# A transformer block on one core: a new opening of the first matrix product, and three due times moved

## The chip, the cores and the metric

The kernel runs on one core of one Trainium2 chip. The time is device microseconds of one launch, from start to end, the median of several runs. Engines are TensorE (PE; its weight loads are shown as PEld), VectorE (DVE), ScalarE (ACT), GpSimd (POOL) and SyncE (SP), which only issues transfers here.

## The reference

One layer on 256 tokens of width 2048: a gated feed-forward part, a mixer, and a second feed-forward part, each with a norm ahead and a norm behind, added to the stream.

```python
f = _swiglu(_rmsnorm(h, ln_ffn1_pre), ffn1_gate, ffn1_up, ffn1_down)
h = h + 0.5 * _rmsnorm(f, ln_ffn1_post)
mx = _hybrid_mixer(_rmsnorm(h, ln_mix_pre), ...)
h = h + _rmsnorm(mx, ln_mix_post)
f = _swiglu(_rmsnorm(h, ln_ffn2_pre), ffn2_gate, ffn2_up, ffn2_down)
h = h + 0.5 * _rmsnorm(f, ln_ffn2_post)
```

The mixer multiplies by `w_in` (columns for an RWKV-7 branch, a pooling branch and two gates). The RWKV branch is a recurrence over tokens with a 64x64 state for each of 16 heads. The pooling branch takes moving means over windows of 2, 4, 8 and 16 tokens, subtracts the input and multiplies each of four groups by a 256x256 matrix (the pool mix). Both branches go through a projection, are gated, added and multiplied by `w_out`. All is float32.

## The kernel before, in words

**Products.** A float32 product is made of three passes at the reduced type fp32r: each operand is split into a high part (ACT casts it: `wH`, `xH`) and the remainder (DVE subtracts: `wL`, `xL`), and TensorE adds H·H, L·H and H·L (lines 155 to 157, function `mm3`). One call of `mm3` for one slice k of 128 rows of the weight, 512 columns of output and one half h (128 tokens) is called a step here ("do" in the code). A product with 2048 rows has 16 slices and two halves, 32 steps. Weights come by SP in tiles of two slices (`get_w`, line 117), are split by `two` (lines 131 and 132), and the split tiles have five buffers; the loaded ones have four. Where the output is wanted transposed, 256-column matmuls are used (`ch_g`, line 311, tile name `mc`).

**Activations.** The right-hand sides must have the channel on the partition axis. `transpose_split` turns a 128x512 block of one half by four TensorE transposes against the identity (line 339, tile `tr`); ACT scales and casts each quarter (line 345) and DVE takes the remainder (line 347). Block c of half h serves slices 4c to 4c+3 of that half.

**The head** (`head`, called by the first `gemm_tok`) is the first product of the first feed-forward part. There the order on TensorE, ACT, DVE and SP is written out by hand: `load(h, c)` asks for a block of x, `load(None, None)` for the norm's gain row g1, which TensorE turns into a column; `get(k, n)` asks for weights, `split(k)` splits them, `turn(h, c)` is `transpose_split`, `do(k, h)` is a step. All asks are in SP's queue.

**Row ends.** `post` makes the last product of each part, then the norm behind it. In the last row of four (c = 3) its steps are queued half by half, with events put among them by their due times on a planned clock (`s.at`, `s.now`; `run` executes the queue). After half h ends, DVE multiplies the four quarters by the norm's factor and adds the stream (line 450, tile `fg`), and each quarter is then turned for the next part. `TURNS[h][q]` is the planned delay, in us after the half's end, of the transposes of quarter q. Steps of the next part's first product (`by_half`, half 0 first, ten slices) are queued behind and fill the time. `TURNS` is used after the first feed-forward part and after the mixer; after the last part there is nothing to turn.

**The mixer** orders TensorE by hand, the other engines' order is chosen by a scheduler. `rwkv` is a generator that yields numbers: how many us of other products (`fill`, from `rest`) are to be woven in at that place (`weave`); what one place draws more than it asked for is taken off the next. It runs for two halves of the heads. `fill` begins with what is left of `p_g`: the steps of a gate (`gb_g(1)`), of which 22 come ahead of the mix of the fourth pool group, `pool_mix(3)`, which needs `mxT` (split by ACT, line 751, and DVE, line 752) and its own weight. The recurrence has four chunks of 64 tokens: `pU`, copied by ACT; `pSa`, copied by DVE and ACT (lines 1044 and 1045); `pS`, from which DVE makes the next state (lines 1055 and 1056) that the next chunk's `pU` needs; and `pY`. Between pSa and pS stands `yield 1.7`. After the last chunk `pT` turns the result, which DVE and ACT split into yH and yL; the first 16 steps of the projection that follows use the other half's.

Of the kernel before, what the change touches and what calls it, by code (L numbers as in the profile page):

```python
# [18 lines left out]
P = 128  # L19
# [21 lines left out]
STAG = 10  # L41
TRAIL = 16
AHEAD = (5.0, 6.0)
TURNS = [[4.2, 5.3, 6.4, 7.5], [4.0, 5.0, 6.2, 7.4]]
TB = 4

ROWS = [("ln_mix_pre", 16), ("ln_ffn2_pre", 16), ("mu", 26), ("w0", 8), ("a0", 8),
# [4 lines left out]
class Block:  # L52
# [154 lines left out]
    def head(s, w, c0, KT, do, keep, xs):  # L207

        load, turn = xs
        w32 = {}  # L210

        def get(k, n):
            w32[k] = (n, s.get_w(w, k, n, c0, 512, own=True))

        def split(k):
            n, t = w32[k]
            keep(s.two(t, k, n, 512))
        E = mybir.EngineType
        with s.tc.manual_schedule(engines={E.PE, E.Activation, E.DVE, E.SP}):
            load(None, None)  # L220
            load(0, 0)
            get(0, 1)
            get(1, 1)
            load(1, 0)
            get(2, 1)
            get(3, 1)
            for c in range(1, 4):
                load(0, c)
                get(4 * c, 2)
                load(1, c)  # L230
                get(4 * c + 2, 2)
            split(0)
            turn(0, 0)
            split(1)
            do(0, 0)
            turn(1, 0)
            split(2)
            do(1, 0)
            split(3)
            do(0, 1)  # L240
            do(1, 1)
            do(2, 0)
            do(2, 1)
            for c in range(4):
                k = 4 * c
                if c < 3:
                    turn(0, c + 1)
                    split(k + 4)
                if c:
                    for i in range(3):  # L250
                        do(k + i, 0)
                        do(k + i, 1)
                        if c < 3 and i == 1:
                            turn(1, c + 1)
                            split(k + 6)
                elif c < 3:
                    turn(1, c + 1)
                    split(k + 6)
                do(k + 3, 0)
                do(k + 3, 1)  # L260
            s.stats()

    def stats(s):
# [90 lines left out]
    def turn(s, T1, h, src):  # L354

        s.nc.vector.transpose(out=T1[:, h * 512:h * 512 + 512], in_=src)  # L356
# [46 lines left out]
    def post(s, wd, at, KT, gpost, fac, resid, emit, reload):  # L403
# [11 lines left out]
        for c in range(4):  # L415
# [32 lines left out]
            def out(h, q, r, end):  # L448
                o = cc_(fg[h], q)
                nc.vector.scalar_tensor_tensor(out=o, in0=o, scalar=r, in1=resid(h, q),  # L450
                                               op0=ALU.mult, op1=ALU.add)
                emit(h, q, o, end + TURNS[h][q])
            s.gemm_tok(wd, c * 512, at, KT, ev, trail=(c == 3))
# [96 lines left out]
    def mixer(s, prm, uT, rs, resid, emit, gpost, reload):  # L550
        nc = s.nc
# [13 lines left out]
        for h in range(2):  # L565
            t = s.tmp("rb")
            nc.vector.tensor_copy(t[:, :P], rs[h].to_broadcast([P, P]))
            ps = s.psum("rb")
# [73 lines left out]
        def p_g():  # L642
            mix = None
            for g, win in enumerate(POOL_WINDOWS):
                mxT = s.unit((P, 2, 2, S), F32R, "mxT")
                yield from s.pool_window(g, win, at, w_in, mxT)
                if g:
                    yield from s.pool_mix(g - 1, mix, prm["pool_w"], pT)
                mix = mxT
            yield None  # L650
            gate = gb_g(1)
            for t in itertools.islice(gate, 22):
                yield t
            yield from s.pool_mix(3, mix, prm["pool_w"], pT)
            yield from gate
# [116 lines left out]
    def rwkv(s, hf, z, lz, prm, yH, yL):  # L772
        nc = s.nc
# [32 lines left out]
        k, v = z["k"], z["v"]  # L806
# [8 lines left out]
        for q in range(2):  # L815
            ps = s.psum("pw").rearrange("p (i t) -> p i t", i=2)
# [5 lines left out]
        for q in range(2):  # L822
            ps = s.psum("pa").rearrange("p (i t) -> p i t", i=2)
# [25 lines left out]
        ps = s.psum("pn")  # L849
# [16 lines left out]
        for pr in range(2):  # L866
            yield 3
            pss = []
            for src in (v, vs):
                ps = s.psum("pV").rearrange("p (i c) -> p i c", i=4)  # L870
# [3 lines left out]
            for b in range(2):  # L874
                c = 2 * pr + b
# [4 lines left out]
        for q in range(2):  # L880
            ps = s.psum("pk").rearrange("p (i t) -> p i t", i=2)
# [44 lines left out]
        for q in range(2):  # L926
            ar, bk = AR[q], BK[q]
            for i in range(2):
# [8 lines left out]
                for h, R, RK in ((0, E, O), (1, O, E)):  # L937
                    ps = pAs[h]
# [59 lines left out]
        ps = s.psum("pM").rearrange("p (g t) -> p g t", g=16)  # L998
# [8 lines left out]
        ps = s.psum("pX").rearrange("p (g t) -> p g t", g=16)  # L1007
# [18 lines left out]
        for c in range(NCH):  # L1026
            yield 1.8 if c else 2.8
            pu = v4(s.psum("pU"))
            for i in range(4):
                for R, h, ev in ((E, 0, EVs), (O, 1, ODs)):  # L1030
                    T.matmul(pu[R, i], AR[i // 2][h][:, i % 2, c, 0], ev[:, i, c],  # L1031
                             start=True, stop=True)
            eo = ((c + 1) % 2) * 512
            ea_ = s.R[0][:, eo:eo + 512].rearrange("p (h i t) -> p h i t", h=2, i=4)
            G.tensor_copy(ea_[O, 0], EVs[O, :, c])
            G.tensor_copy(ea_[E, 1], ODs[E, :, c])
            us = s.rtmp("us").rearrange("p (i t) -> p i t", i=4)
            A.copy(us, pu)
            yield 1.6
            pa = v4(s.psum("pSa"))  # L1040
            for i in range(4):
                for R in (E, O):
                    T.matmul(pa[R, i], tt[R, i * NCH + c], us[R, i], start=True, stop=True)  # L1043
            V.tensor_copy(ea_[E, 0], pa[E])
            A.copy(ea_[O, 1], pa[O])
            yield 1.7
            if c < NCH - 1:
                pS = v4(s.psum("pS"))
                for i in range(4):
                    for R, h in ((E, 0), (O, 1)):  # L1050
                        T.matmul(pS[R, i], BKt[i // 2][:, i % 2, c, h], ea_[:, h, i],  # L1051
                                 start=True, stop=True)
                st = s.rtmp("st").rearrange("p (i t) -> p i t", i=4)
                for R, ev in ((E, EVs), (O, ODs)):
                    V.tensor_tensor(out=st[R], in0=pS[R], in1=ev[R, :, c], op=ALU.add)
                    V.tensor_tensor(out=ev[R, :, c + 1], in0=st[R],
                                    in1=lc4[R, :, c:c + 1].to_broadcast([64, 4, C]),
                                    op=ALU.mult)
            py = v4(s.psum("pY"))
            for i in range(4):  # L1060
                for R, h, ev in ((E, 0, EVs), (O, 1, ODs)):
                    T.matmul(py[R, i], AR[i // 2][h][:, i % 2, c, 1], ev[:, i, c],  # L1062
                             start=i == 0, stop=False, skip_group_check=True)
            for i in range(4):
                for R, h in ((E, 0), (O, 1)):
                    T.matmul(py[R, i], Xrb[R, i * NCH + c], ea_[R, h, i],  # L1066
                             start=False, stop=i == 3, skip_group_check=True)
            s1 = s.small(4, "g1", bufs=2)
            V.tensor_reduce(out=s1, in_=py, axis=AX.X, op=ALU.add)
            V.tensor_scalar(out=s1, in0=s1, scalar1=1.0 / HD, scalar2=None, op0=ALU.mult)  # L1070
            yc = yn[:, :, c]
            V.tensor_tensor(out=yc, in0=py, in1=s1.unsqueeze(2).to_broadcast([P, 4, C]),
                            op=ALU.subtract)
            ysq = s.rtmp("ysq").rearrange("p (i t) -> p i t", i=4)
            A.activation(out=ysq, in_=yc, func=AF.Square)
            s2 = s.small(4, "g2", bufs=2)
            V.tensor_reduce(out=s2, in_=ysq, axis=AX.X, op=ALU.add)
            V.tensor_scalar(out=s2, in0=s2, scalar1=1.0 / HD, scalar2=GN_EPS,
                            op0=ALU.mult, op1=ALU.add)
            s3 = s.small(4, "g3", bufs=2)  # L1080
            G.tensor_tensor(out=s3, in0=s2, in1=s.mhalf[:, :4], op=ALU.pow)
            V.tensor_tensor(out=yc, in0=yc, in1=s3.unsqueeze(2).to_broadcast([P, 4, C]),
                            op=ALU.mult)
# [31 lines left out]
def kernel(tc, x, ln_ffn1_pre, ln_ffn1_post, ffn1_gate, ffn1_up, ffn1_down,  # L1115
# [4 lines left out]
    nc = tc.nc  # L1120
# [6 lines left out]
    with ExitStack() as ctx:  # L1127
        s = Block(tc, ctx)
        xs = [[s.unit(p="x") for _ in range(2)] for _ in range(2)]

        def at_tok(u):
            return lambda h, c: u[h][c // 2][:, (c % 2) * 512:(c % 2) * 512 + 512]
# [4 lines left out]
        def load(h, c):  # L1137
            if h is None:
                nc.sync.dma_start(out=gr, in_=ln_ffn1_pre[0].rearrange("(k p) -> k p", p=P))
                ps = s.psum("pg1")  # L1140
                nc.tensor.transpose(ps[:, :16], gr, s.ident[:16, :16])
                nc.vector.tensor_copy(g1, ps[:, :16])
                return
            nc.sync.dma_start(out=at_tok(xs)(h, c),
                              in_=x[0, h * P:h * P + P, c * 512:c * 512 + 512])

        def turn(h, c):
            pre(h, c, at_tok(xs)(h, c))
# [65 lines left out]
```

## Time and profile before

| | |
|---|---|
| median of 3 runs | 2104.89 us (2104.62, 2104.89, 2106.89) |
| the profiled execution | 2106.46 us |
| its span, first to last instruction | 2104.8 us |
| PE busy | 2085.8 us (99%) |
| DVE, ACT, POOL busy | 1255.8, 1116.2, 73.5 us |
| mean granted TensorE clock | 0.998 |

Times in rows are microseconds from the span's start. A row of the timeline has start, duration, engine, line, operation, tiles and count, and in brackets how long the engine had been idle and what ended that. A matmul's duration includes its drain, so matmuls overlap: their pace is read from their starts. A row of the waits has the waiting engine and line, what it waited for, the total, how often and the longest. A row of the windows view has the stretch, its length, busy time and number of instructions of PE, PEld, DVE, ACT and POOL, the granted clock, the share of DMA time and GB/s.

### The profile page before, as it was taken

How to read it: one execution, taken by the hardware profiler on the slowest of the kernel's cores; microseconds unless marked ns; L12 is line 12 of the kernel's file. 1: busy time of each engine (PE TensorE's matmuls, PEld its weight loads, DVE VectorE, ACT ScalarE, POOL GpSimd, SP SyncE). 2: the span in 40 equal slices, each digit the busy share in tenths (PEclk: the TensorE clock that was granted, in tenths of full speed). 3: DMA queues.
4: the chain of work that ended last, by engine and by line, in shares of the span. 5: the costliest groups of instructions: out<-in, count | busy, mean ns of one | idle time of the engine just before them, and what ended most of it. 6: DMA issues, size and time to landing. Idle time of an engine off the chain costs nothing.

```text
span 2104.8 us, 28799 instructions
## 1 busy us (share of the span) xinstructions
PE 2085.8 (99%) x11077; PEld 1758.1 (84%) x11077; DVE 1255.8 (60%) x1588; ACT 1116.2 (53%) x1600; POOL 73.5 (3%) x161
## 2 busy tenths in 40 slices
PE   8999999999999999999999999999999999999998
PEld 7888888888888889989988788888888888888886
DVE  6555555555444565799789666565555555554444
ACT  6565555655444465465465444365655566554442
POOL 0000000000000010000110110000000000000000
PEclk9999999999999999999999999999999999999999
DMA  7656666567666666655456575566666666676564
GB/s 250 192 179 209 193 197 192 176 218 245 194 195 192 191 195 189 177 174 171 135 154 194 151 261 182 196 213 194 180 205 197 193 191 186 208 247 196 192 193 138
DMA packets 224116, 406.99 MB, mean 193 GB/s; under 512 B 13151, under 2 KB 49129, under 8 KB 223977
## 3 DMA queue, kind: packets, MB, share of 16 engines
q1 hardware_dynamic: 218089, 385.21, 59.3%
q0 software_dynamic: 5888, 19.93, 2.6%
q8 instruction: 87, 1.43, 0.3%
q14 instruction: 52, 0.43, 0.1%
HBM read 396.69 MB, written 8.39 MB: 192 GB/s over the span
## 4 chain that ended last, share of the span: by engine, by line
PE 90%; issue 8%; DVE 1%; DMA 0%; POOL 0%; ACT 0%; POOLq 0%; DVEq 0%; SPq 0%; ACTq 0%
PE mm L155 26%; PE mm L157 25%; PE mm L156 25%; PE mc L311 10%; PE pA L935 0%; PE tr L339 0%; DMA mb<-msp 0%; PE pU L1031 0%; PE pY L1066 0%; PE pSa L1043 0%; DVE fg L450 0%; PE pY L1062 0%; PE pM L1001 0%; PE pS L1051 0%; DMA x<-in_x_dram 0%
## 5 line engine op out<-in xcount | busy, mean ns | idle before, releaser
L132 DVE TENSOR_TENSOR wL<-w,wH 128x1024 fp32r<-128x1024 f32 (+2 forms) x725 | 872.9, 1212 | 742.8 <-ACT wH L131 741.5
L131 ACT CAST wH<-w 128x1024 fp32r<-128x1024 f32 (+2 forms) x725 | 753.0, 1047 | 823.2 <-PE mm L157 667.6
L155 PE MATMUL mm<-wH,xH 128*128 128x512 f32 x2460 | 962.6, 392 | 0.5 <-ACT xH L345 0.5
L156 PE MATMUL mm<-wL,xH 128*128 128x512 f32 x2460 | 958.8, 390 | 0.9 <-DVE wL L132 0.9
L157 PE MATMUL mm<-wH,xL 128*128 128x512 f32 x2460 | 958.8, 390 | 0.0
L155 PEld LDWEIGHTS mm<-wH,xH 128*128 128x128 f32 x2460 | 462.7, 188 | 96.8 <-ACT xH L345 0.9
L157 PEld LDWEIGHTS mm<-wH,xL 128*128 128x128 f32 x2460 | 462.5, 188 | 96.9 <-DVE xL L347 0.6
L156 PEld LDWEIGHTS mm<-wL,xH 128*128 128x128 f32 x2460 | 462.8, 188 | 95.6 <-DVE wL L132 1.5
L311 PE MATMUL mc<-xH,wH 128*128 128x256 f32 x560 | 159.6, 285 | 0.0
L311 PE MATMUL mc<-xL,wH 128*128 128x256 f32 x560 | 158.4, 283 | 0.0
L311 PE MATMUL mc<-xH,wL 128*128 128x256 f32 x560 | 158.3, 283 | 0.0
L366 ACT COPY x<-T 32x256 f32<-32x256 f32 x352 | 142.4, 405 | 3.9
L311 PEld LDWEIGHTS mc<-xH,wH 128*128 128x128 f32 x560 | 105.9, 189 | 1.0
L311 PEld LDWEIGHTS mc<-xH,wL 128*128 128x128 f32 x560 | 106.0, 189 | 0.3
L311 PEld LDWEIGHTS mc<-xL,wH 128*128 128x128 f32 x560 | 106.0, 189 | 0.1
L385 ACT ACTIVATE sg<-mm,rs 128x512 f32<-128x512 f32 x44 | 29.9, 690 | 21.5 <-PE mm L157 21.5
L386 DVE SCALAR_TENSOR_TENSOR sg<-mm,rs,sg 128x512 f32<-128x512 f32 x44 | 31.5, 751 | 8.4 <-ACT sg L385 8.4
L373 ACT ACTIVATE junk<-mm 128x512 bf16<-128x512 f32 x24 | 14.5, 606 | 38.0 <-PE mm L157 38.0
L418 POOL DMA_DIRECT2D gb<-in_ln_ffn_post_dram x4 | 2.4, 593 | 891.5 <-DVE xL L370 858.1
L356 DVE STREAM_TRANSPOSE T<-sg 128x512 f32<-128x512 f32 x44 | 30.9, 703 | 0.0
L391 DVE SCALAR_TENSOR_TENSOR sg<-mm,rs,sg 128x512 f32<-128x512 f32 x44 | 30.9, 745 | 0.0
L345 ACT ACTIVATE xH<-tr,cols 128x128 fp32r<-128x128 f32 x64 | 18.1, 391 | 16.7 <-PE tr L339 16.7
(243 smaller groups left out, 1074.8 us busy)
## 6 DMA issues: line engine op xcount, KB each, us to landing
w<-in_ffn_up_dram SPq DMA_DIRECT2D x176, 512.0 KB
w<-in_ffn_down_dram SPq DMA_DIRECT2D x176, 512.0 KB
w<-in_ffn_gate_dram SPq DMA_DIRECT2D x174, 512.0 KB
w<-in_w_in_dram SPq DMA_DIRECT2D x128, 512.0 KB
w<-in_w_out_dram SPq DMA_DIRECT2D x32, 512.0 KB
w<-in_w_proj_b_dram SPq DMA_DIRECT2D x16, 512.0 KB
w<-in_w_proj_a_dram SPq DMA_DIRECT2D x16, 512.0 KB
hsp<-fg POOLq DMA_DIRECT2D x16, 256.0 KB, 3.5
```

Source lines behind the costliest of these rows:

```text
L131: s.nc.scalar.copy(vH, v)
L132: s.nc.vector.tensor_tensor(out=vL, in0=v, in1=vH.bitcast(F32), op=ALU.subtract)
L155: nc.tensor.matmul(ps, aH, bH, start=start, stop=False)
L156: nc.tensor.matmul(ps, aH, bL, start=False, stop=False)
L157: nc.tensor.matmul(ps, aL, bH, start=False, stop=stop)
L311: s.nc.tensor.matmul(o, lh, rh, start=one and n == 0, stop=k == KT - 1 and n == 2, skip_group_check=True)
L345: nc.scalar.activation(out=dH[:, i], in_=ps[:, i], func=AF.Copy, scale=g)
L356: s.nc.vector.transpose(out=T1[:, h * 512:h * 512 + 512], in_=src)
L366: nc.scalar.copy(dst[q * 32:q * 32 + 32, :, :, i], src[i * 32:i * 32 + 32, :, :, q])
L385: nc.scalar.activation(out=sg, in_=ps, func=AF.Sigmoid, scale=rs[h])
L386: nc.vector.scalar_tensor_tensor(out=sg, in0=ps, scalar=rs[h], in1=sg, op0=ALU.mult, op1=ALU.mult)
L391: nc.vector.scalar_tensor_tensor(out=sig[h], in0=ps, scalar=rs[h], in1=sig[h], op0=ALU.mult, op1=ALU.mult)
```

## The change

Four edits. In the head, TensorE begins with twelve transposes of the identity into a PSUM bank that nobody reads; the first blocks of x for both halves are asked for by ACT's queue (ahead of its table load) instead of SP's; both are turned before the first step, and the steps then run slice by slice, both halves each, with the next block's transposes after slices 0, 2, 4 and so on. `TURNS` for half 1 is later in its first three quarters. `pool_mix(3)` comes after 27 gate steps instead of 22. `yield 1.7` between pSa and pS becomes 2.2. All four due times count on TensorE alone; the scheduler orders ACT and DVE anew around them.

```diff
-TURNS = [[4.2, 5.3, 6.4, 7.5], [4.0, 5.0, 6.2, 7.4]]
+TURNS = [[4.2, 5.3, 6.4, 7.5], [5.3, 6.0, 6.7, 7.4]]
+WARM = 12
...
         with s.tc.manual_schedule(engines={E.PE, E.Activation, E.DVE, E.SP}):
+            ps = s.psum("warm")
+            for _ in range(WARM):
+                s.nc.tensor.transpose(ps[:, :P], s.ident, s.ident)
+            load(0, 0)
+            load(1, 0)
             load(None, None)
-            load(0, 0)
             get(0, 1)
             get(1, 1)
-            load(1, 0)
             get(2, 1)
...
             split(0)
             turn(0, 0)
             split(1)
-            do(0, 0)
             turn(1, 0)
             split(2)
-            do(1, 0)
             split(3)
-            do(0, 1)
-            do(1, 1)
-            do(2, 0)
-            do(2, 1)
-            for c in range(4):
...
+            for k in range(KT):
+                do(k, 0)
+                do(k, 1)
+                if k % 2 == 0 and k + 4 < KT:
+                    turn(k // 2 % 2, k // 4 + 1)
                     split(k + 4)
...
-            for t in itertools.islice(gate, 22):
+            for t in itertools.islice(gate, 27):
...
-            yield 1.7
+            yield 2.2
...
-            nc.sync.dma_start(out=at_tok(xs)(h, c),
-                              in_=x[0, h * P:h * P + P, c * 512:c * 512 + 512])
+            (nc.sync if c else nc.scalar).dma_start(
+                out=at_tok(xs)(h, c), in_=x[0, h * P:h * P + P, c * 512:c * 512 + 512])
```

## The prediction

> **What bounds the kernel now.** I read the page's first part, then the waits of PE, then the timeline around each of them.
>
> ```profile
> PE 2085.8 (99%) x11077; PEld 1758.1 (84%) x11077; DVE 1255.8 (60%) x1588; ACT 1116.2 (53%) x1600; POOL 73.5 (3%) x161
> ...
> PE tr L339 <- DVE fg L450: 2.3, 2, 1.2
> PE tr L339 <- DMA x<-in_x_dram: 2.1, 1, 2.1
> PE mc L311 <- DVE mxT L752: 1.8, 1, 1.8
> PE pS L1051 <- ACT R L1045: 0.9, 1, 0.9
> ...
> SPq L117 <- DVE wL L132: 1524.8, 640, 13.4
> ```
>
> TensorE sets the time; behind the head it waits in four places only: twice 1.2 us at row ends, 1.8 at the pool mix, 0.9 in the recurrence. The change goes to these and to the head. SP waits for buffers that DVE frees, not for data, so weights follow TensorE when it comes earlier. A step (three 512-column matmuls, "do") takes 0.68 us: 737.16 to 737.84 below, by 0.227 a matmul.
>
> **Head.**
>
> ```profile
> 1.26 0.41 SPq L1144 DMA_DIRECT2D x<-in_x_dram  x1
> ...
> 1.38 0.29 POOL masks.py:199 TENSOR_SCALAR_AFFINE_SELECT ident<-ident 128x128 f32<-128x128 f32 x1
> ...
> 4.88 1.11 PE L339 MATMUL tr<-ident,x 128*128 128x128 f32 x4 [2.07 <-DMA x<-in_x_dram]
> ...
> 5.54 0.62 ACT L131 CAST wH<-w 128x512 fp32r<-128x512 f32 x1 [3.46 <-DMA w<-in_ffn_gate_dram]
> ...
> 6.07 1.14 ACT L345 ACTIVATE xH<-tr,g 128x128 fp32r<-128x128 f32 x4
> ...
> 6.48 0.79 PE L155 MATMUL mm<-wH,xH 128*128 128x512 f32 x1 [0.49 <-ACT xH L345]
> ...
> 6.19 0.69 DVE L132 TENSOR_TENSOR wL<-w,wH 128x512 fp32r<-128x512 f32 x1 [3.16 <-ACT wH L131]
> ...
> 7.24 1.13 DVE L347 SCALAR_TENSOR_TENSOR xL<-tr,g,xH 128x128 fp32r<-128x128 f32 x4 [0.35 <-ACT xH L345]
> ...
> 10.80 0.61 PE L156 MATMUL mm<-wL,xH 128*128 128x512 f32 x1
> ...
> 11.22 0.42 PE L157 MATMUL mm<-wH,xL 128*128 128x512 f32 x1
> ...
> 11.48 0.40 PE L155 MATMUL mm<-wH,xH 128*128 128x512 f32 x1
> ...
> 11.71 0.39 PE L156 MATMUL mm<-wL,xH 128*128 128x512 f32 x1
> ...
> 26.71 0.60 PE L339 MATMUL tr<-ident,x 128*128 128x128 f32 x4
> ...
> 27.07 0.48 PE L155 MATMUL mm<-wH,xH 128*128 128x512 f32 x1
> ...
> 4.40:7.85 3.45, 2.48 (x7) 1.50 (x7) 1.30 (x4) 2.17 (x6) 0.00 (x0) 1.00 1.00 360
> ```
>
> Matmuls start 0.42 us apart until 11.22 and 0.23 apart from 11.48: the array is at half rate up to about 11.2. (The last row, of the windows view, shows a clock of 1.00; I go by the spacing.) Twelve steps of 0.68 follow the last transposes, so the head's row of 32 steps ends near 27.07 + 12 x 0.68 + 0.1 = 35.4.
>
> The change issues both first x blocks from ACT, at about 0.8 and 1.25 by SP's 0.41 an issue, and SP's weights come one slot (0.45) earlier. No row shows an ACT queue. By SP's rows a block is usable 3.6 after its issue, and at 360 GB/s a 256 KB block takes 0.73. x0, w0, w1, x1 were usable near 4.9, 5.5, 6.3 and 7.0. Now the four share the rate and are all there by about 7.0 - 0.45, call it 6.4 (bounds: 5.8 if ACT's queue adds rate, 7.0 if the lead is lost). TensorE's order in the built kernel is 12 transposes from about 1.75 (ident is made at 1.67), at most 1.11 / 4 = 0.28 each and so done by 5.1, hidden under the wait for x; the g1 transpose; tr(0,0), tr(1,0); then both halves of each k. ACT: cast 5.3 to 5.9, xH to 7.0, second cast to 7.6, xH of half 1 to 8.7. DVE: xL of half 0 7.05 to 8.2, wL to 8.85, xL of half 1 from 8.85, its first block at 9.15. So the first matmul comes at 7.3, after 6.48 before, but then nothing stands. At half rate k=0 ends at 9.9, tr(0,1) at 10.75; with full rate from 11 on k=1 ends at 12.4, k=2 13.75, tr 14.2, k=3 15.55, and 24 steps and four sets of transposes (0.36, and 0.1 in the matmul behind) later 33.75: a gain of 1.6. If the array is fast from 8, half 1 waits for xL (9.15) and the end is 32.6: 2.75. The lag from first work to full rate was 11.2 - 4.9 counted from transposes, 11.2 - 6.5 from matmuls; that gives 8.0 or 12.0 now. I take 10, a gain of **2.1**, bounds 0.7 (blocks at 7.0, fast at 12) to 3.3 (blocks at 5.8, fast at 8).
>
> By the Trainium skill, "TensorE: Matmul & The Clock Gate", Part 4 (PE-mode transpose), transposes do not count as busy for the clock: the twelve would buy nothing, 12.0 would hold and the head gain 1.3. The rows above do not settle it.
>
> **Row ends** (twice, alike).
>
> ```profile
> 737.16 0.39 PE L155 MATMUL mm<-wH,xH 128*128 128x512 f32 x1
> ...
> 738.35 2.74 DVE L450 SCALAR_TENSOR_TENSOR fg<-fg,rs,xr 128x512 f32<-128x512 f32 x4
> ...
> 739.16 0.66 PE L339 MATMUL tr<-ident,fg 128*128 128x128 f32 x4 [1.16 <-DVE fg L450]
> ...
> 741.03 4.51 DVE L347 SCALAR_TENSOR_TENSOR xL<-tr,cols,xH 128x128 fp32r<-128x128 f32 x16
> ```
>
> The last step before the transposes ends at 737.84, they start at 739.16: 1.32 lost. In the order of the built kernel eight steps stand ahead of them instead of six, 1.36 us, so they start at 739.2, when fg is there. The second to fourth stand together one step later; fg's fourth quarter (741.1) meets the fourth at 741.2. One step later, at 742.45, half 1 of the row begins; its xL is being made from 741.03 on, the first of 16 parts in 0.28. **1.3 each, 2.6** for both; bounds 2.0 to 2.8.
>
> **Pool mix.**
>
> ```profile
> 916.11 0.28 PE L311 MATMUL mc<-mxT,wH 128*128 128x256 f32 x1
> ...
> 916.95 0.28 PE L311 MATMUL mc<-mxT,wL 128*128 128x256 f32 x1
> ...
> 919.03 0.65 PE L311 MATMUL mc<-mxT,wH 128*128 128x256 f32 x2 [1.80 <-DVE mxT L752]
> ...
> 923.23 1.04 PE L885 MATMUL pk<-ident,R 128*128 128x128 f32 x8
> ...
> 918.55 0.42 DVE L752 TENSOR_TENSOR mxT<-pl,mxT 128x256 fp32r<-128x256 f32 x1
> ...
> 915.80:919.20 3.40, 1.60 (x12) 1.31 (x11) 3.33 (x7) 1.33 (x3) 0.00 (x0) 1.00 0.36 132
> ...
> 919.22:922.62 3.40, 3.40 (x11) 2.81 (x11) 3.34 (x5) 1.59 (x4) 0.00 (x0) 0.50 0.33 102
> ```
>
> mxT's remainder comes late on DVE, behind products that prepare the state. TensorE stands from 917.19 to 919.03, 1.84, and for the next 3.4 us the granted clock is 0.50: 1.7 more. Five more gate steps, and the eight pk transposes that now come first (0.8 to the next start, 1.04 with the drain), put the mix at 916.11 + 5 x 0.68 + 0.8 = 920.3. DVE gets there later too: in the built order a full weight tile (1.23, as at 1196.21 below) takes the place of the pool weight's half one (0.69, as at 6.19) ahead of it, so mxT is done near 918.97 + 0.54 = 919.5, and the pool weight's remainder, now behind it, at 920.15, when the second matmul asks for it at 920.4. No wait: **1.84 and 1.7**. Bounds: 2.5 (a wait of 1 us stays, too short to take the clock) and 3.6.
>
> The Trainium skill, "TensorE: Matmul & The Clock Gate", Part 1 (The HAM clock gate), lets the clock drop after an idle window of some 3.4 us and asks for no gaps over about 3 us; here 1.84 of standing was enough, and by the rule the 1.7 would not belong to this wait. The rows decide.
>
> The 1.7 also places the profiled execution: it took 2106.46, 1.66 over its span, and the runs shown are 2104.62, 2104.89 and 2106.89. Two are 1.7 below it, as if the drop comes in some executions only. So I take 2106.46 less all terms; against the median of 2104.89 the 1.7 is no gain.
>
> **Recurrence.**
>
> ```profile
> 1194.54 0.69 PE L1051 MATMUL pS<-R,R 128*64 128x64 f32 x16
> ...
> 1196.21 1.23 DVE L132 TENSOR_TENSOR wL<-w,wH 128x1024 fp32r<-128x1024 f32 x1
> ...
> 1197.35 0.86 DVE L1056 TENSOR_TENSOR R<-st,lc 64x256 f32<-64x256 f32 x2
> ...
> 1198.52 0.69 PE L1031 MATMUL pU<-R,R 128*64 128x64 f32 x16
> ...
> 1029.34 1.05 ACT L131 CAST wH<-w 128x1024 fp32r<-128x1024 f32 x1 [2.52 <-PE mc L311]
> ...
> 1026.95 0.69 PE L1051 MATMUL pS<-R,R 128*64 128x64 f32 x16
> ...
> 1233.16 2.08 PE L1102 MATMUL pT<-ident,R 64*64 64x64 f32 x64
> ...
> 1239.32 0.69 DVE L1111 TENSOR_TENSOR yL<-R,yH 128x512 fp32r<-128x512 f32 x1
> ```
>
> The half microsecond more (1.7 to 2.2) puts a step more ahead of most pS; the one wait of 0.9 goes. But in the built order a weight remainder now stands on DVE ahead of the state update L1056 in all six cycles that have one; before it did in one, the one quoted. There the state was ready 3.7 after pS and pU came at 3.98, behind three steps. Two cycles of the second half now have two steps there, pU at 3.3: 0.45 lost each; one of the first half loses 0.1. Net **-0.1**, bounds -1.5 and +0.9. Six fill steps that stood behind pT are used up earlier: 16 steps (10.9 us) still stand between pT (end 1235.2) and the first use of yL (1240.0); without them 4.8 would show.
>
> **Sum**: 2.1 + 2.6 + 1.84 + 1.7 - 0.1 = 8.1; 2106.46 - 8.1 = **2098.3**, 6.6 below the median shown.
>
> **Rivals.** (a) The array counts only matmuls: fast at 12, head 1.3, 2099.1. For it: the window 4.40 to 7.85, busy 2.48, was not enough. (b) Transposes count: fast at 8, head 2.75, 2097.7. (c) Blocks are late: all eight queued transfers share one rate, and with both transposes ahead of the first matmul the head gains nothing: 2098.3 + 2.1 = 2100.4. For it: x takes 3.6 to land and all depends on it; against it: the bytes ahead of the fourth block are the same as before. (d) The mix is not cured: DVE's chain moves along with it and the wait and the clock drop stay: 2098.3 + 3.5 = 2101.8. For it: the pool weight's remainder now stands behind mxT, with 0.25 of room; against it: only a shift of DVE by 1.5 more would bring back a wait long enough to take the clock. (e) Slower: the weight remainder ahead of the state update. In the cycle at 1026.95 the cast came 2.39 after pS, since the buffer was freed late; with the remainder in front, the state would be ready at 2.4 + 1.05 + 1.2 + 0.9 = 5.55, and pU, asking at 3.3 to 4.0, would stand 1.6 to 2.25, in six cycles 11.5: 2109.8. It decides from a cast 1.2 after pS on, and eats the 6.6 with waits of 1.1, from a cast at 1.6 on. Against it: the extra step frees the buffer when pS starts.
>
> **How the numbers follow.** Forecast 0.50, own range 2097.0 to 2099.8; (a) 0.15, (b) 0.12, (c) 0.11, (d) 0.08, (e) 0.04. The range 2096.0 to 2101.6 holds all but (e), half of (d) and the outer ends of the bounds. 0.2% (4.2 us) is about what a measurement tells from no change. Faster than 2100.7: forecast, (a), (b), half of (c), 0.83; within: the rest of (c) and (d), 0.13; slower 0.04.
>
> **What would show it.** Right: PE's waits have no L339 behind L450 and no L311 behind L752, clock 1.00 around 920, the head's row ends near 33.3 (35.4 before), pU waits under 0.5 behind L1056 in two cycles. Wrong: first x transposes after 5.5 or the second pair after 7.5 (c), a clock of 0.50 anywhere inside, waits of pU over 1 us (e), or a wait in a place where there was none.

## The result and the profile after

| | median, us | range | runs |
|---|---|---|---|
| before, run beside it | 2106.31 | 2104.62 to 2107.32 | 15 |
| changed | 2100.37 | 2100.02 to 2104.45 | 15 |
| forecast | 2098.3 | 2096.0 to 2101.6 | |

The ratio is 0.9978, with a 95% interval of 0.997 to 0.9986. Against its own yardstick, the profiled execution of before (2106.46), the profiled execution of the changed kernel took 2100.07 (span 2098.4): 6.4 gained where the sum said 8.1. The medians moved by 5.9; both mix executions with and without a drop of the clock, which "The clock drop" and "The sum" below take apart.

The page's first line (busy us, share of the span, instructions):

```profile
PE 2085.2 (99%) x11089; PEld 1758.4 (84%) x11089; DVE 1254.1 (60%) x1588; ACT 1111.3 (53%) x1600; POOL 74.3 (4%) x161
```

PE's busy time is the same but for 0.6; idle time was 19.0 (2104.8 - 2085.8) before and is 13.2 now. These are net figures: the slow 3.4 us behind the mix count as busy in before, and the twelve new transposes (2.8) count as busy in the changed kernel. The waits of PE in the changed kernel (what waited, for what, us in total, times, longest):

```profile
PE mm L156 <- ACT sgb L547: 1.8, 1, 1.8
PE warm L223 <- POOL ident masks.py:199: 1.7, 1, 1.7
PE mm L158 <- DVE xL L334: 0.7, 2, 0.5
PE pSa L1030 <- ACT us L1025: 0.4, 1, 0.4
PE tr L326 <- DMA x<-in_x_dram: 0.4, 1, 0.4
```

(Line numbers behind the head are 13 lower than before.) All four waits that the prediction went for are gone: no transposes behind fg, no mix behind mxT, no pS behind R. But there is a wait in a place where there was none: a step, L156, stands 1.8 us for ACT's sgb, the sigmoid of a gate.

To see where the 6.4 came from, compare the start of instructions that stand at the same place of PE's order in both traces (as many matmuls ahead of them, but for the twelve new transposes). Timeline of before, then of the changed kernel:

```profile
725.83 0.60 PE L339 MATMUL tr<-ident,fg 128*128 128x128 f32 x4
...
913.18 0.60 PE L872 MATMUL pV<-ident,zv 128*128 128x128 f32 x4
...
941.92 1.27 PE L935 MATMUL pA<-R,R 64*128 64x128 f32 x18
...
1261.83 1.03 PE L339 MATMUL tr<-ident,sga 128*128 128x128 f32 x8
...
2096.44 0.39 PE L157 MATMUL mm<-kH,xL 128*128 128x512 f32 x1
```

```profile
723.46 0.60 PE L326 MATMUL tr<-ident,fg 128*128 128x128 f32 x4
...
909.45 0.60 PE L859 MATMUL pV<-ident,zv 128*128 128x128 f32 x4
...
936.68 1.50 PE L922 MATMUL pA<-R,R 64*128 64x128 f32 x22
...
1256.81 1.03 PE L326 MATMUL tr<-ident,sga 128*128 128x128 f32 x8
...
2090.04 0.39 PE L158 MATMUL mm<-kH,xL 128*128 128x512 f32 x1
```

The leads are 2.37, 3.73, 5.24, 5.02 and 6.40. Their differences are the account of the change, for these two executions:

| part | forecast | account |
|---|---|---|
| head | 2.1 | 2.37 |
| first row end | 1.3 | 1.36 |
| pool mix, with the clock drop | 3.54 | 1.51 |
| recurrence | -0.1 | -0.22 |
| second row end | 1.3 | 1.38 |
| sum | 8.1 | 6.40 |

One row of this table is off, and by more than the whole error. The timeline of the changed kernel around the mix shows why:

```profile
915.29 0.43 DVE L739 TENSOR_TENSOR mxT<-pl,mxT 128x256 fp32r<-128x256 f32 x1
...
916.57 0.36 PE L298 MATMUL mc<-mxT,wH 128*128 128x256 f32 x1
...
917.07 2.36 DVE L133 TENSOR_TENSOR wL<-w,wH 128x1024 fp32r<-128x1024 f32 x2
...
918.09 0.40 PE L156 MATMUL mm<-wH,xH 128*128 128x512 f32 x1
...
919.35 1.28 DVE L873 TENSOR_TENSOR R<-R,pk 128x512 f32<-128x512 f32 x2
920.54 0.68 DVE L908 TENSOR_TENSOR R<-zr,R 64x512 f32<-64x512 f32 x1
921.15 0.47 DVE L752 SCALAR_TENSOR_TENSOR yb<-mc,cols,yb 128x256 fp32r<-128x256 f32 x1
...
921.51 0.39 PE L156 MATMUL mm<-wH,yb 128*128 128x512 f32 x1
...
921.65 0.47 ACT L751 ACTIVATE yb<-mc,cols 128x256 fp32r<-128x256 f32 x1 [0.71 <-DVE yb L752]
...
921.97 0.39 PE L158 MATMUL mm<-wH,yb 128*128 128x512 f32 x1
922.14 1.28 ACT L547 ACT_TABLE_LOAD   x1
923.44 1.26 ACT L547 ACTIVATE sgb<-mm,rs 128x512 f32<-128x512 f32 x2
924.18 0.50 PE L156 MATMUL mm<-wH,yb 128*128 128x512 f32 x1 [1.82 <-ACT sgb L547]
```

mxT is done at 915.72 and the mix starts at 916.57, right behind pk: no wait, as forecast. Behind the mix only five gate steps are left (918.09 to 921.5); then the next product (wH, yb) begins. A product needs one bank of PSUM, the memory in which TensorE adds it up, for each half of the tokens, and the four banks of the pool are given out in turn. Its first half finds a free PSUM bank. Its second half does not: of the four banks the gate holds two, the mix one, the product's first half the fourth, so the second half takes over the bank of the gate's first half, which is empty only when ACT has read it out as sgb. And ACT is late: its second yb waits until 921.62 for DVE's first, which stands behind two weight remainders and the state's products; then comes the table load of the sigmoid, 1.28, and only then sgb. In before the same dependence was there, with ten steps in between:

```profile
923.66 0.47 ACT L764 ACTIVATE yb<-mc,cols 128x256 fp32r<-128x256 f32 x1
...
927.46 1.28 ACT L560 ACT_TABLE_LOAD   x1
928.75 1.27 ACT L560 ACTIVATE sgb<-mm,rs 128x512 f32<-128x512 f32 x2
...
929.59 0.39 PE L155 MATMUL mm<-wH,yb 128*128 128x512 f32 x1
```

There the second yb was done 3.3 us before the table load, sgb started as the gate ended, and its first half (done by 929.4) was out when the second half of the product asked at 929.59. So the five steps that were put ahead of the mix to cover one wait had been covering another.

### The profile page after: what moved, and what is told of

Read it like the earlier page. It is cut to its first block, busy times and chain, and to the rows that moved or that the text cites. A ratio compares the mean times of both kernels' runs of the same rounds, so it can differ in the third digit from the quotient of the medians.

```text
span 2098.4 us, 28820 instructions
## 1 busy us (share of the span) xinstructions
PE 2085.2 (99%) x11089; PEld 1758.4 (84%) x11089; DVE 1254.1 (60%) x1588; ACT 1111.3 (53%) x1600; POOL 74.3 (4%) x161
## 4 chain that ended last, share of the span: by engine, by line
PE 97%; DVE 1%; issue 1%; ACT 0%; DMA 0%; DVEq 0%; POOLq 0%; POOL 0%; SPq 0%; ACTq 0%
PE mm L156 28%; PE mm L158 28%; PE mm L157 28%; PE mc L298 10%; PE tr L326 1%; PE pA L922 0%; DVE wL L133 0%; PE pSa L1030 0%; PE pU L1018 0%; DMA w<-in_ffn_gate_dram 0%; PE pT L1089 0%; PE pM L988 0%; PE pb L951 0%; PE pS L1038 0%; PE pY L1053 0%
## 5 line engine op out<-in xcount | busy, mean ns | idle before, releaser
L156 PE MATMUL mm<-wH,xH 128*128 128x512 f32 x2460 | 961.7, 392 | 0.0
L156 PEld LDWEIGHTS mm<-wH,xH 128*128 128x128 f32 x2460 | 462.0, 188 | 96.0 <-ACT xH L332 0.4
L156 PE MATMUL mm<-wH,yb 128*128 128x512 f32 x64 | 26.0, 407 | 1.8 <-ACT sgb L547 1.8
```

What stands on the lines that cost most here:

```text
L156: nc.tensor.matmul(ps, aH, bH, start=start, stop=False)
```

## Experiments

All times are medians with their range; "before" was run again beside each group of four (2105.65 in 26 runs, 2106.50 in 30, 2105.73 in 14), and the intervals of the ratios are against those.

| run | what differs | median, us | range | runs | ratio, 95% |
|---|---|---|---|---|---|
| e1 | changed, mix in another bank | 2098.12 | 2097.76 to 2098.49 | 5 | 0.9949 to 0.9976 |
| e2 | changed, mix edit undone | 2101.43 | 2099.96 to 2103.79 | 11 | 0.9970 to 0.9988 |
| e3 | changed, recurrence edit undone | 2100.41 | 2099.70 to 2102.32 | 10 | 0.9967 to 0.9985 |
| e4 | changed, no transposes of the identity | 2102.33 | 2100.02 to 2104.14 | 11 | 0.9972 to 0.9989 |
| e5 | before, mix edit alone | 2106.29 | 2105.14 to 2107.25 | 11 | 0.9993 to 1.0010 |
| e6 | before, row ends alone | 2102.70 | 2102.22 to 2104.04 | 11 | 0.9979 to 0.9996 |
| e7 | changed, ACT's order at the mix | 2099.41 | 2098.77 to 2099.85 | 8 | 0.9961 to 0.9982 |
| e8 | changed, x on SP's queue | 2102.53 | 2100.51 to 2103.09 | 11 | 0.9974 to 0.9992 |
| e9 | e1 with the old head | 2100.57 | 2100.27 to 2101.11 | 10 | 0.9965 to 0.9984 |
| e10 | e1, no transposes of the identity | 2099.00 | 2098.67 to 2099.67 | 5 | 0.9956 to 0.9981 |
| e11 | e1, recurrence edit undone | 2097.99 | 2097.61 to 2099.66 | 5 | 0.9952 to 0.9977 |
| e12 | e1, four more transposes | 2098.06 | 2098.00 to 2099.52 | 5 | 0.9951 to 0.9978 |

**e1: is it the bank?** The edit leaves ACT and DVE as they are, so it separates the bank from the lateness.

```diff
-    def ch_g(s, w, c0, cw, at, KT, evac, kstep):
+    def ch_g(s, w, c0, cw, at, KT, evac, kstep, bank=None):
...
-        banks = [s.pm.tile([P, 512], F32, tag="mm", name=s.nm("mc"))
+        banks = [bank() if bank else s.pm.tile([P, 512], F32, tag="mm", name=s.nm("mc"))
...
-                          2)
+                          2, (lambda: s.psum("mc")) if g == 3 else None)
```

> The changed kernel with one thing different: the last pool mix accumulates in a bank of the other PSUM pool (the one of the transposes), so that the first product behind the gate finds two free banks. Theory A (bank): the 1.8 us wait at 924 is the product's second half waiting for the bank of the gate's first half, which ACT empties late; then no step waits behind sgb, everything from 924 on comes 1.8 to 2.0 earlier, and the time is 2098.2 (2098.0 to 2098.5), in profile and in most runs. Rival B (ACT late for others too): ACT's and DVE's lateness around 921 meets the next reader instead, a wait of 0.8 us or more shows elsewhere between 922 and 945, and the time is 2099.3 to 2100.2.

2098.12. The waits of PE (first fence) and the timeline (second) of this run:

```profile
PE warm L223 <- POOL ident masks.py:199: 1.7, 1, 1.7
PE tr L326 <- DMA x<-in_x_dram: 0.6, 1, 0.6
PE pSa L1030 <- ACT us L1025: 0.4, 1, 0.4
```

```profile
921.65 0.47 DVE L752 SCALAR_TENSOR_TENSOR yb<-mc,cols,yb 128x256 fp32r<-128x256 f32 x1
...
922.16 0.47 ACT L751 ACTIVATE yb<-mc,cols 128x256 fp32r<-128x256 f32 x1 [0.66 <-DVE yb L752]
...
922.47 0.39 PE L158 MATMUL mm<-wH,yb 128*128 128x512 f32 x1
922.65 1.28 ACT L547 ACT_TABLE_LOAD   x1
922.69 0.39 PE L156 MATMUL mm<-wH,yb 128*128 128x512 f32 x1
```

ACT waits for DVE and loads its table exactly as late as before (all rows stand 0.5 later, since this execution's head ended 0.5 later), but TensorE goes from the product's first half (922.47) to its second (922.69) without a gap. Theory A holds, B falls: nobody else asks for what ACT is late with. This version beats both kernels.

**e2, e3: which edit made the wait?** e2 sets the mix's 27 back to 22, e3 the recurrence's 2.2 back to 1.7.

> The changed kernel with the pool mix where it was (22 gate steps ahead of it instead of 27), all else as changed. Theory A: the wait behind mxT is back (1.8 us) and the one behind sgb is gone, since ten steps again stand between the mix and the product: 2100.1 in runs without a clock drop, 2101.8 in runs where the clock is 0.50 for 3.4 us behind the wait. Rival C (the wait behind sgb comes from another edit): both waits show, 2101.9 without a drop and 2103.6 with one.

> The changed kernel with the recurrence's fill as it was (1.7 instead of 2.2). Theory A: the wait behind sgb stays at 1.8 us (it lies 100 us ahead of the recurrence); pS waits 0.9 again and pSa no longer 0.4; the recurrence edit was worth -0.2 in the account, so the time is 2099.9 (2099.5 to 2100.4). Rival C: the wait behind sgb goes, 2098.2.

In e2 the wait behind mxT is back (1.8) and none is behind sgb; the runs fall into 2099.96 to 2100.57 (four), 2101.42 to 2101.92 (six) and one of 2103.79, as A has it without and with a clock drop. In e3 the wait behind sgb stays at 1.8; six runs lie at 2099.70 to 2100.54 and four, all with a mean granted clock of 0.998 instead of 0.999, at 2101.31 to 2102.32. The wait belongs to the mix edit; C falls.

**e5: the mix edit alone**, the same 22 to 27 in the kernel before.

> The kernel before with the pool mix's edit alone (27 gate steps ahead of the mix). Theory A: the wait behind mxT (1.8 us) goes and one of 1.8 behind sgb comes, with the clock drop in about half the executions as before: no gain, 2104.9 without a drop, 2106.6 with one, median 2104.6 to 2106.8. The forecast's own step: both the wait and the drop are gone, 2103.0 in all runs.

2106.29, ratio 1.0002: no gain, and the forecast's own 2103.0 is out of reach of every run. Its waits of PE hold the exchange in one line:

```profile
PE mm L155 <- ACT sgb L560: 1.8, 1, 1.8
```

Here too the wait behind mxT is gone. In the profiled execution no drop followed.

**e7: why is the bank late?** The mix's evacuation issues both ACT parts first, then both DVE parts; the bank is as in the changed kernel.

```diff
             for i in range(2):
...
                 nc.scalar.activation(out=yb[:, 0, i], in_=ps, func=AF.Copy, scale=sc)
+            for i in range(2):
+                ps = banks[0][:, i]
+                sc = s.col["pool_scale"][:, 2 * g + i:2 * g + i + 1]
                 nc.vector.scalar_tensor_tensor(out=yb[:, 1, i], in0=ps, scalar=sc,
```

> The changed kernel with the mix's two ACT evacuations (yb) issued ahead of its two DVE ones, so that ACT does not wait for DVE between them; the bank stays. Theory G (the bank is late because ACT stands 0.7 us for DVE and then loads its table): the table load starts at 920.9 instead of 922.1, sgb's first half is done near 922.9, and the wait shrinks to 0.4 to 0.8, too short for a clock drop: 2098.7 to 2099.2 in nearly all runs. Rival H (the late cast of the weights ahead of it sets the table load): the wait stays above 1.4 and the time at 2100.1.

ACT's rows of the timeline, and PE's wait:

```profile
918.77 0.84 ACT L751 ACTIVATE yb<-mc,cols 128x256 fp32r<-128x256 f32 x2 [3.30 <-DVE wL L133]
919.50 2.00 ACT L132 CAST wH<-w 128x1024 fp32r<-128x1024 f32 x2
921.51 1.28 ACT L547 ACT_TABLE_LOAD   x1
```

```profile
PE mm L156 <- ACT sgb L547: 0.7, 1, 0.7
```

This execution's head ended 0.48 later, so 921.51 is 921.03 on the clock of the changed kernel, against 922.14: 1.1 earlier, and the wait is 1.1 shorter. G holds. The rest, 0.7, is the two casts and the table load, which take 3.3 us from 919.5 on. The median, 2099.41, is 0.2 above G's range and 1.29 above e1. Of that the traces show 1.0: from the step at 895.23 in the changed kernel (895.71 in e7, 895.73 in e1) to the sixteen pA matmuls at 947.92 (947.25 and 946.26), past the mix, e7 gains 1.15 on the changed kernel and e1 gains 2.16. TensorE's order is the same in all three. The other 0.3 this run leaves open. No run shows another 1.7 on top.

**e6: the row ends alone**: the kernel before with TURNS of the changed one.

> The kernel before with the row ends' edit alone. The account of the two profiles gives 1.37 for each row end: 2102.2 in runs without a clock drop, 2104.0 with one, and no PE wait behind fg. Rival F (the row ends' gain comes in part from what the head shifted, such as the order of DVE): a wait of 0.3 us or more stays behind fg, 2102.8 and 2104.6.

Eight of eleven runs lie at 2102.22 to 2103.03, three at 2103.52 to 2104.04; no wait behind fg. F falls. The profiled execution had no clock drop and a head 0.58 later than the profile of before (its last transposes at 27.29, 26.71 there): 2104.8 - 1.7 + 0.58 = 2103.7 to its span of 2101.0, 2.7 for two row ends. The runs give less: the middle of the eight is 2102.63, 2.3 below the middle of before's runs with a clock of 0.999 (2104.97). No run settles which of the two holds.

**e9, e4, e10: the head.** e9 is e1 with the head of before; e4 and e10 set WARM to 0 in the changed kernel and in e1.

> The kernel of the first experiment (changed, with the mix in the other bank) with the head as it was before the change. Neither kernel has a wait long enough for a clock drop, so the difference is the head alone. The account of the two profiles gave 2.37, with the clock at full rate from 5.1 after and 11.3 before; over executions with the clock opening at any of its moments: theory K (the forecast's middle, 2.1): 2100.2 (2099.9 to 2100.9). Rival L (the forecast's upper bound, 3.3, since the old head also opens late): 2101.4.

> The changed kernel without the twelve transposes of the identity. Theory D (they open the clock): the clock record shows the full rate from 8.6 or 12.0 (one or two windows of 3.41 us later than 5.1) instead of 5.1, matmuls stand 0.42 apart until then, the head's row of 32 steps ends at 33.3 to 34.1 instead of 33.0, and the time is 2100.4 to 2101.2. Rival E (transposes do not count, as the forecast's rival (a) had it): the full rate begins where it does with them, the head ends at 33.0 and the time is 2100.1.

> The kernel of the first experiment without the twelve transposes. Theory D (they open the clock a window or two earlier): the full rate starts between 8.5 and 13.1, the head's last transposes start 0.6 to 2.0 later than at 26.2, the time is 2098.7 to 2100.2. Rival E (they do not count for the clock): the full rate starts between 8 and 12 with and without them and the time is 2098.1.

The head is worth 2100.57 - 2098.12 = 2.45: theory K. e4 alone would have been hard to read: its runs mix two things, the head and the clock drop behind sgb (its profiled execution had both, 2104.14), and its four runs with a clock of 0.999 spread from 2100.02 to 2101.58. In e10, without a drop, the transposes are worth 2099.00 - 2098.12 = 0.9 of the 2.45. When the trace's clock record shows the full rate, and what the head's last transposes did, over the profiled executions with the new order of the head (e8, with x on the other queue, is told below):

| run | transposes of the identity | full rate from | second x block turned at | last transposes at |
|---|---|---|---|---|
| changed | 12 | 5.14 | 5.90 | 25.70 |
| e2 | 12 | 7.18 | 5.97 | 25.68 |
| e11 | 12 | 10.13 | 6.06 | 26.00 |
| e7 | 12 | 9.89 | 6.25 | 26.18 |
| e1 | 12 | 10.13 | 6.40 | 26.21 |
| e3 | 12 | 10.12 | 7.20 | 26.43 |
| e12 | 16 | 4.72 | 7.36 | 27.20 |
| e10 | 0 | 11.72 | 6.05 | 26.81 |
| e4 | 0 | 13.06 | 7.28 | 28.21 |

The clock record begins with the full rate; for the time ahead of it the windows view shows 1.00, as in the prediction's row 4.40:7.85. With the old head the full rate began at 11.27 (before), 12.73, 12.63 and 12.89 (e5, e6, e9). So with transposes ahead the clock opens at 4.7 to 10.1, without them at 11.3 to 13.1: they count, theory D. In the changed kernel's profiled execution the full rate began at 5.14, before a single matmul other than transposes had run (the first one starts at 6.56).

**e8: whose queue asks for x?** Only the line of the first blocks' queue differs (SP for ACT).

> The changed kernel with the first two x blocks asked for on SP's queue, as the others. Theory I (the second queue buys one SP slot each, 0.4 us, for the weights): x comes at 4.9 and 5.3 to 6.0, the first weights two slots (0.8) later than now, the head ends 0.3 to 0.8 later: 2100.4 to 2100.9 without a drop. Rival J (the transfers share one rate whatever the queue): no difference, 2100.0 to 2100.3.

The least of its runs is 0.5 above the least of the changed kernel (2100.51 and 2100.02), and its profiled head has the full rate from 8.82 and the last transposes at 26.09, inside the table's 25.7 to 26.4 with twelve transposes. Six of its eleven runs have a mean granted clock of 0.997 or 0.998, so the median does not decide; I and J stay open.

**e11: the recurrence without the noise**: e1 with 1.7.

> The kernel of the first experiment with the recurrence's fill as it was (1.7). The forecast gave the recurrence's edit -0.1, the account -0.2, that is a small loss: then 2097.9 to 2098.0 without it. Rival M (the edit does what it is for: pS's 0.9 is gone and pSa's 0.4 comes, and steps ahead are worth the rest): 2098.6.

2097.99, 0.13 below e1, and the ranges overlap: no gain from the edit, and M falls. The traces put its cost at 0.2: from the sixteen pA matmuls named under e7 to the sga transposes, across the recurrence, e1 takes 308.88 (946.26 to 1255.14) and e11 308.65 (946.05 to 1254.70), the changed kernel 308.89 (947.92 to 1256.81) and e3 308.65 (948.61 to 1257.26).

**e12: filling the gap in the head.** Behind the transposes of the first x block, four more of the identity:

```diff
             turn(0, 0)
+            for _ in range(4):
+                s.nc.tensor.transpose(ps[:, :P], s.ident, s.ident)
             split(1)
             turn(1, 0)
```

> The kernel of the first experiment with four more transposes of the identity between the transposes of the first and those of the second x block, where TensorE stood 0.6 us. Theory N (the clock opens after the first window of 3.41 us that is filled, wherever the windows stand): full rate from 5.1 to 8.6 in every execution, the last transposes of the head at 25.7 or earlier, 2097.6 to 2098.0 in all runs. Rival O (the four hold up the second block's transposes where it lands early, and the DVE remainders set the pace anyway): 2098.1 to 2098.6.

2098.06, the same as e1. The profiled execution was the slowest of the five (2099.52). In it the clock opened at 4.72, the earliest of all, but the second x block landed late, and everything followed it:

```profile
7.36 0.66 PE L328 MATMUL tr<-ident,x 128*128 128x128 f32 x4 [1.57 <-DMA x<-in_x_dram]
```

The early clock is what N asked for, but one execution does not show it for every one, and the median lies between N's range and O's: neither is decided. Over the table both scatter from one execution to the next, the landing of the second block (5.9 to 7.4) and the opening of the clock.

## Why the prediction was off, step by step

**What bounds the kernel**: right. TensorE set the time, and the waits named were the ones that went.

**Head**, 2.1 forecast, 2.37 by the account, 2.45 by e9: right in size, and inside its bounds, but not along its path, so in part by luck. The rows of the changed kernel's head:

```profile
5.90 0.66 PE L326 MATMUL tr<-ident,x 128*128 128x128 f32 x4 [0.36 <-DMA x<-in_x_dram]
6.56 0.50 PE L156 MATMUL mm<-wH,xH 128*128 128x512 f32 x1
...
7.71 0.50 PE L158 MATMUL mm<-wH,xL 128*128 128x512 f32 x1 [0.20 <-DVE xL L334]
...
9.35 0.50 PE L158 MATMUL mm<-wH,xL 128*128 128x512 f32 x1 [0.51 <-DVE xL L334]
```

The blocks came earlier than the 6.4 assumed, the first matmul at 6.56 instead of 7.3, and the clock was open at 5.14 instead of 10. But "then nothing stands" was wrong: the matmuls wait for the remainders of x (0.7 in all). Nor is there one lag from the first work to the full rate, as the prediction took it: with one and the same head the full rate began anywhere from 5.14 to 10.13. Rival (b), transposes count, had the mechanism, with the xL of half 1 as the limit: it gave 2.75. Rival (a) is contradicted by the clock record and by e10. So is the rule of the Trainium skill behind it ("TensorE: Matmul & The Clock Gate", Part 4, PE-mode transpose: a transpose does not count as busy for the clock). Rival (c), late blocks, had a second pair after 7.5 as its sign; no profiled execution shows that, the latest are 7.28 (e4) and 7.36 (e12).

**Row ends**, 1.3 each forecast, 1.36 and 1.38 by the account, 2.3 for both by e6's runs, inside the bounds of 2.0 to 2.8: right, and for the reason given. The last step ahead of the transposes and the quarter of fg that they need, in the timeline of the changed kernel:

```profile
735.98 2.74 DVE L437 SCALAR_TENSOR_TENSOR fg<-fg,rs,xr 128x512 f32<-128x512 f32 x4
...
736.61 0.39 PE L158 MATMUL mm<-wH,xL 128*128 128x512 f32 x1
736.83 0.61 PE L326 MATMUL tr<-ident,fg 128*128 128x128 f32 x4
```

**Pool mix**, 1.84 and 1.7 forecast, 1.51 measured: here the prediction failed. Its sentence "No wait: 1.84 and 1.7" followed DVE only, ahead of the mix: is mxT there, is the pool weight there. It costed five steps moved ahead as a gain of cover and did not ask what they had covered where they stood. The steps between the mix and the next product went from ten to five (6.8 to 3.4 us), while ACT needed, from the end of the mix (918.25) to the end of sgb's first half (923.44 + 0.63), 5.8. The new wait took 1.82 of idle time, 1.98 by the starts (the next start came 2.21 behind the last, not 0.23), and 3.54 - 1.98 = 1.56 is near the 1.51 of the account. e5 shows the edit alone is worth nothing. None of the rivals had it; "a wait in a place where there was none" was only named among the signs.

**The clock drop** (the granted clock halved for 3.4 us): its 1.7 was gained in the profiled execution, but not for the reason given (no wait long enough): the new wait is as long as the old one. Busy time of PE (second number behind the width, then PEld, DVE, ACT, POOL) and granted clock (behind POOL) in stretches of 3.41 us, counted on from the start of full rate, first in the changed kernel, then in e4, then in e3:

```profile
919.92:923.33 3.41, 2.44 (x11) 1.69 (x9) 3.37 (x9) 2.68 (x3) 0.23 (x1) 1.00 0.79 260
923.33:926.74 3.41, 2.56 (x11) 2.11 (x12) 3.40 (x5) 2.64 (x7) 0.30 (x1) 1.00 0.09 36
```

```profile
924.42:927.83 3.41, 1.58 (x7) 0.98 (x6) 3.37 (x6) 3.38 (x5) 0.53 (x1) 1.00 0.40 153
927.83:931.24 3.41, 3.41 (x10) 2.63 (x9) 3.37 (x8) 1.57 (x4) 0.00 (x0) 0.50 0.44 154
```

```profile
921.48:924.89 3.41, 1.60 (x8) 0.98 (x6) 3.37 (x7) 2.75 (x5) 0.53 (x1) 1.00 0.70 246
924.89:928.30 3.41, 3.39 (x15) 2.82 (x16) 3.37 (x7) 2.69 (x5) 0.00 (x0) 1.00 0.24 54
```

In the changed kernel's profiled execution the edge between two stretches cuts the wait in two, 0.97 and 0.85 idle, and nothing follows. In e4 the same wait lies within one stretch, 1.83 idle, and the next runs at 0.50, as in before. In e3 it lies within one stretch too, 1.81 idle, and the next runs at full rate. So a wait within one stretch can bring the drop and need not; PE's busy time does not tell the cases apart (1.58 and 1.60 with a drop in e4 and before, 1.60 without one in e3), and what does stays open. The drop remained possible in the changed kernel: five of its fifteen runs are 1.5 to 4.2 above the middle of the other ten (2100.24), and these five have a mean granted clock of 0.997 or 0.998 where the ten have 0.999. None of the five was profiled; a drop explains up to 1.7 of each, and what the largest have beyond it is not shown. With e1, where no such wait is left, all five runs lie within 0.8, at a clock of 0.999.

**Recurrence**, -0.1 forecast, -0.22 by the account, -0.24 by e3's trace, -0.23 by e11's and -0.13 by its median: right in sign and near in size, but not by its parts. pS waits no longer, pSa waits 0.4 for ACT, which the prediction did not have, and pU, which was to lose 0.45 in each of two cycles, loses 0.08 in each (0.40 from the last start to its own instead of 0.32): rival (e) did not come. What the remaining tenths are lies in small gaps that were not followed.

**The sum.** With the mix at its measured 1.51 the prediction's own terms give 2.1 + 2.6 + 1.51 - 0.1 = 6.1, that is 2100.4. Runs without a drop say the same: the prediction put its time 6.6 below such a run of before, and from 2104.97 to 2100.24 (the middles of the runs with a clock of 0.999) it is 4.7; the 1.9 that is missing is about the new wait (1.98). With the bank freed, e1, the mix gains 3.67 on before in the traces (1.51 and 2.16) where 3.54 was forecast, and the time is 2098.12 where 2098.3 was forecast. The forecast was that of a kernel with one more edit; that it fits so closely owes something to the head and the recurrence, whose sizes were right for other reasons.

## What to carry to other kernels

When steps are pulled ahead to cover a wait, look at both ends: what stood behind them, who reads out the banks they leave, and how long that engine needs, its table loads and its own waits included. A pool of four banks in rotation ties a product to the evacuation of the bank given out four allocations earlier; the dependence doesn't show in a profile as long as it is covered, so it has to be counted from the allocations. And where a clock drop comes in some executions only, take the wait that brings it away first, then compare: e4 and e8 could not be read, e10 could.

## What the runs showed of the hardware

The edges of the clock's windows keep their step over the whole execution: from the start of full rate to the edge of the drop it is 907.95 us in before (11.27 to 919.22) and 914.77 in e4 (13.06 to 927.83), 266 and 268 steps of 3.4133 us. The Trainium skill, "TensorE: Matmul & The Clock Gate", Part 1, gives a free-running window of 3413 ns; the traces agree. Where the edges stand against the program differs in each execution.

One wait of 1.8 us costs 1.8 in some executions and some 3.5 in others: of 85 runs of before, 39 lie around 2104.97 and 46 around 2106.88 (the middle of each group), and where the record has the mean granted clock of a run it is 0.999 in all 32 of the lower group and 0.998 in all 38 of the upper. No wait of 3.4 us was needed for the drop: 1.8 idle in one window was enough in two profiled executions (before, e4). It was not in a third (e3, 1.81), nor was 1.66 in a fourth (e2), and 0.97 and 0.85 in two windows was not either (changed kernel). So it does not hang on this alone whether the wait lies in one window.

The landing of one 256 KB block at the start of the program scatters by 1.5 us between executions of kernels that ask for it alike (the second x block is turned at 5.90 to 7.36). In the two executions with the clock open before it, the changed kernel and e12, that scatter goes straight through the head: 1.46 between the blocks, 1.50 between the last transposes (25.70 and 27.20).
